# Storing 1100 output columns in the middle of the load queue of a max-pool kernel

## The chip, the cores and the metric

The kernel runs on one core of one Trainium2 chip. The metric is device time in microseconds (us), with a granted clock of 1.0. "Profile" is the page of one profiled execution, "trace" the records behind it, and "packet records" the trace's list of DMA packets with start, duration and size. Times inside an execution are counted from the start of its span, and each run has one profiled execution. The "SP ring" and the "ACT ring" are the queues of the DMAs (transfers) that these two engines issue; the buffer that the kernel calls `ring` is something else. A "row" is one partition's part of a transfer, and is one packet in the records. A "turn" is the place where the stream of loads changes to a store, or back.

## The reference

The reference is an adaptive max pool. With 32 x 256 rows of 4096 floats and 256 outputs per row, each output is the maximum of 16 neighbouring values: 134.22 MB are read, 8.39 MB written.

```python
def reference(x, output_size):
    batch, channels, length = x.shape
    result = np.zeros((batch, channels, output_size), dtype=np.float32)
    for i in range(output_size):
        start = int(i * length / output_size)
        end = int((i + 1) * length / output_size)
        result[:, :, i] = np.max(x[:, :, start:end], axis=-1)
    return result
```

## The kernel before

The outputs form two groups. Each group is spread over 128 partitions and loaded in pieces of up to 1024 windows (16 floats each) into a ring buffer that holds two pieces. VectorE reduces each piece in two parts, 876 (in one piece 872) and 148 columns. The larger is always first: the next load into the same half of the buffer needs its place and not that of the smaller. Results stay on chip in `kept`, and are stored at the end; only the last 836 columns go out on ACT's ring.

```python
    ring = pool.tile([P, 2 * (CHUNK + GAP) * W], fp32, tag="ring", name="ring")
    kept = pool.tile([P, total - last], fp32, tag="kept", name="kept")
    # ... cut ...
    for g, loads in enumerate((group_a, group_b)):
        xg, og = group(sum(loads))
        # ... cut: a first load of 192 windows ...
                low = n_loads % 2 * (CHUNK + GAP)
                moved = n_loads // 2 % 2
                at = low + moved * GAP
                nc.sync.dma_start(out=ring[:, at * W : (at + n) * W], in_=xn)
                # ... cut: pooled(...) of the two parts, or of the last piece ...
                n_loads += 1
            a += n
        full = a - last if g else a
        stores.append((og[:, 0:full], kept[:, base : base + full]))
        base += full

    nc.scalar.dma_start(out=og[:, full : full + last], in_=last_kept)
    tc.no_sync_barrier()
    for dst, src in stores:
        nc.sync.dma_start(out=dst, in_=src)
```

"The eighth load" below is the eighth of the 1024-window loads, the first load of 192 windows not counted.

Of the kernel before, what the change touches and what calls it, by code (L numbers as in the profile page):

```python
# [1 line left out]

# [4 lines left out]


@with_exitstack
def kernel(  # L10
    ctx: ExitStack,
    tc: tile.TileContext,
    x: bass.AP,
    output_size: bass.AP,
    out: bass.AP,
):








    nc = tc.nc
    P = nc.NUM_PARTITIONS
    fp32 = mybir.dt.float32

    B, C, L = x.shape
    O = int(output_size)  # L30
    assert L % O == 0, (L, O)
    W = L // O
    total = B * C * O // P
    assert B * C * O % P == 0

    CHUNK = 1024
    GAP = 148
    FIRST = 192
    LOADS_A, LOADS_B = 9, 6

    LESS = 4
    group_a = [FIRST] + [CHUNK] * (LOADS_A - 1) + [CHUNK - LESS]
    last = total - sum(group_a) - LOADS_B * CHUNK
    group_b = [CHUNK] * LOADS_B + [last]
    assert 0 < last and last * (W + 1) <= CHUNK * W

    pool = ctx.enter_context(tc.tile_pool(name="pool", bufs=1))
    ring = pool.tile([P, 2 * (CHUNK + GAP) * W], fp32, tag="ring", name="ring")
    kept = pool.tile([P, total - last], fp32, tag="kept", name="kept")

    xw = x.flatten_outer_dims().rearrange("r (o w) -> (r o) w", w=W)
    ow = out.flatten_outer_dims().rearrange("r o -> (r o)")

    def pooled(dst, at, n):

        nc.vector.reduce_max(  # L56
            out=dst,
            in_=ring[:, at * W : (at + n) * W].rearrange("p (n w) -> p n w", w=W),
            axis=mybir.AxisListType.X,
        )  # L60

    taken = 0

    def group(n):

        nonlocal taken
        span = slice(taken * P, (taken + n) * P)
        taken += n
        return (
            xw[span].rearrange("(p n) w -> p (n w)", p=P),  # L70
            ow[span].rearrange("(p n) -> p n", p=P),
        )

    stores = []
    n_loads = 0
    base = 0
    for g, loads in enumerate((group_a, group_b)):
        xg, og = group(sum(loads))
        a = 0
        for n in loads:  # L80
            xn = xg[:, a * W : (a + n) * W]
            dst = kept[:, base + a : base + a + n] if n != last else None
            if n == FIRST:

                nc.sync.dma_start(  # L85
                    out=ring[:, CHUNK * W : (CHUNK + n) * W], in_=xn
                )
                pooled(dst, CHUNK, n)
            else:
# [5 lines that stand above are left out]
                if n != last:  # L95
                    cut = CHUNK - GAP if moved else GAP
                    parts = [(0, cut), (cut, n)]
                    for u, v in parts if moved else parts[::-1]:
                        pooled(dst[:, u:v], at + u, v - u)
                else:  # L100
                    end = (at + CHUNK) * W
                    last_kept = ring[:, end - n : end]
                    pooled(last_kept, at, n)
                n_loads += 1
            a += n
        full = a - last if g else a
        stores.append((og[:, 0:full], kept[:, base : base + full]))
        base += full
    assert taken == total

# [6 lines that stand above are left out]
# [1 line left out]
_INS = ['x', 'output_size']  # L118
_OUTS = [((32, 256, 256), 'float32')]

_NUMBERS = {'output_size': 256}


# [26 lines left out]
```

## Time and profile before

| | before |
|---|---|
| time, median | 335.06 us (6 runs, 334.91 to 335.16) |
| DMA share from 20 to 330 us | 1.00, at 432 to 433 GB/s |
| VectorE busy | 276.5 us, 83% |
| first packet of the small store after ACT's issue (packet records) | 1.88 us |
| last packet of all (packet records) | 331.92 us |

The prediction shows most of the lines. The timeline of VectorE: the columns are start, duration, engine, line, operation, output and input with shapes, count, and in brackets the idle time before it and what ended it.

```profile
142.35 17.28 DVE L56 TENSOR_REDUCE kept<-ring 128x876 f32<-128x14016 f32 x2 [2.08 <-DMA ring<-in_x_dram]
161.70 17.28 DVE L56 TENSOR_REDUCE kept<-ring 128x876 f32<-128x14016 f32 x2 [2.07 <-DMA ring<-in_x_dram]
180.97 17.21 DVE L56 TENSOR_REDUCE kept<-ring 128x872 f32<-128x13952 f32 x2 [1.99 <-DMA ring<-in_x_dram]
```

The second line is the eighth load's reduce, the third the ninth's. VectorE waits about 2 us for each load. As the SP ring is never idle, any longer wait here means that the loads themselves came later.

The ninth load in the chain of waits (start, length, what), and what the SP queue waits for at its end (total, times, longest):

```profile
157.13 23.82 DMA ring<-in_x_dram
```

```profile
SPq L145 <- DMA out_dram<-kept: 16.7, 1, 16.7
SPq L145 <- DMA out_dram<-ring: 1.0, 1, 1.0
```

The last two lines say that the large stores land first and the small one 1.0 us after them.

### The profile page before, as it was taken

Reading aid. Unit: us, or ns where it says so; the run is one execution under the profiler, and the core shown is the slowest. Engines: PE = TensorE matmul, PEld = TensorE weight load, DVE = VectorE, ACT = ScalarE, POOL = GpSimd, SP = SyncE. Lnnn points to the kernel's source line nnn. Section 1 sums busy time; section 2 is a strip of 40 time slices with the busy share of each in tenths; the row PEclk is TensorE's granted clock in tenths of the full one; section 3 lists DMA queues with packets and bytes.
Section 4 is the critical chain, followed back from the end, with each engine's and each line's share of the span. In section 5 each row is a group of like instructions: output and inputs, shape, how many; then the busy total and the mean of one; then the engine's idle time right before and its main releaser. Section 6 shows DMA issues by size and latency. Waiting matters only on the chain.

```text
span 333.3 us, 114 instructions
## 1 busy us (share of the span) xinstructions
DVE 276.5 (83%) x32; POOL 0.2 (0%) x4
## 2 busy tenths in 40 slices
DVE  1208979798897979899797979979797997979994
POOL 0000000000000000000000000000000000000000
DMA  8989898998989898999989898999989898989997
GB/s 315 503 378 503 378 496 385 456 425 385 496 378 503 378 503 378 480 401 409 470 376 502 378 503 378 488 393 425 456 378 503 378 503 378 488 353 494 405 401 317
DMA packets 2880, 142.61 MB, mean 428 GB/s; under 512 B 320, under 2 KB 320, under 8 KB 448
## 3 DMA queue, kind: packets, MB, share of 16 engines
q1 hardware_dynamic: 2736, 142.18, 98.8%
q10 hardware_dynamic: 144, 0.43, 0.3%
HBM read 134.22 MB, written 8.39 MB: 428 GB/s over the span
## 4 chain that ended last, share of the span: by engine, by line
DMA 58%; DVE 36%; DVEq 5%; issue 0%; SPq 0%
DMA ring<-in_x_dram 58%; DVE kept L56 36%; DVEq L145 5%; SPq L85 0%
## 5 line engine op out<-in xcount | busy, mean ns | idle before, releaser
L56 DVE TENSOR_REDUCE kept<-ring 128x148 f32<-128x2368 f32 (+3 forms) x31 | 262.5, 8507 | 51.9 <-DMA ring<-in_x_dram 51.9
L56 DVE TENSOR_REDUCE ring<-ring 128x836 f32<-128x13376 f32 x1 | 14.1, 14076 | 0.0
L131 POOL MEMSET const-bfloat16-1.0<- 128x1 bf16 x1 | 0.1, 102 | 0.0
L131 POOL MEMSET const-uint8-127<- 128x1 uint8 x1 | 0.1, 102 | 0.0
L131 POOL MEMSET const-float32-0.0<- 128x1 f32 x1 | 0.1, 99 | 0.2 <-issue 0.2
L131 POOL MEMSET const-float32-1.0<- 128x1 f32 x1 | 0.1, 99 | 0.0
## 6 DMA issues: line engine op xcount, KB each, us to landing
ring<-in_x_dram SPq DMA_DIRECT2D x1, 8160.0 KB, 23.8
ring<-in_x_dram SPq DMA_DIRECT2D x1, 6688.0 KB, 20.4
out_dram<-kept SPq DMA_DIRECT2D x1, 4702.0 KB, 31.2
out_dram<-kept SPq DMA_DIRECT2D x1, 3072.0 KB, 17.0
ring<-in_x_dram SPq DMA_DIRECT2D x1, 1536.0 KB, 6.2
out_dram<-ring ACTq DMA_DIRECT2D x1, 418.0 KB, 4.1
ring<-in_x_dram SPq DMA_DIRECT2D x14, 23.9
```

What stands on the lines that cost most here:

```text
L56: nc.vector.reduce_max(out=dst, in_=ring[:, at * W : (at + n) * W].rearrange("p (n w) -> p n w", w=W), axis=mybir.AxisListType.X,)
L131: nc = _bacc.Bacc("TRN2", target_bir_lowering=False, num_devices=1)
L145: with _tile.TileContext(nc) as tc:
```

## The change

Its intent is evidently to shorten the stores of the tail, by writing 1100 columns (563 KB) while the loads still run.

```diff
+    EARLY, EARLY_AT = 1100, 8
     for g, loads in enumerate((group_a, group_b)):
 ... cut ...
                 n_loads += 1
+                if n_loads == EARLY_AT:
+                    nc.sync.dma_start(out=og[:, 0:EARLY], in_=kept[:, 0:EARLY])
             a += n
         full = a - last if g else a
-        stores.append((og[:, 0:full], kept[:, base : base + full]))
+        done = EARLY if g == 0 else 0
+        stores.append((og[:, done:full], kept[:, base + done : base + full]))
         base += full
```

## The prediction

> **What bounds the kernel now.** I read the page's busy shares first, then the busy time of engines and DMA in three stretches, then the chain of work that ended last, the timeline of the tail, the groups by shape, and last the packet records of the trace.
>
> ```profile
> DVE 276.5 (83%) x32; POOL 0.2 (0%) x4
> ...
> q1 hardware_dynamic: 2736, 142.18, 98.8%
> q10 hardware_dynamic: 144, 0.43, 0.3%
> HBM read 134.22 MB, written 8.39 MB: 428 GB/s over the span
> ```
>
> One compute engine works, VectorE (DVE), at 83% of the span. The load ring q1 carries nearly all bytes, at 98.8% of sixteen DMA engines over the whole span. The next view tells whether the missing 1.2% lies inside the stream or at its ends. Columns: stretch in us, its length, DVE busy, POOL busy, clock, DMA share, GB/s.
>
> ```profile
> 20.00:312.00 292.00, 256.76 (x30) 0.00 (x0) 1.00 1.00 433
> 312.00:330.00 18.00, 16.35 (x2) 0.00 (x0) 1.00 1.00 432
> 328.00:334.00 6.00, 0.35 (x1) 0.00 (x0) 1.00 0.51 211
> ```
>
> From 20 us to 330 us the DMA share is 1.00 at 432 to 433 GB/s, in the loads as in the stores of the tail. What is missing is at the start and after 330 us. The forty-slice row with its 7s, 8s and 9s is misleading here: short slices count a packet as a lump, and longer stretches even this out.
>
> ```profile
> 258.37 14.76 DVE kept L56
> 273.13 0.02 issue
> 273.15 23.91 DMA ring<-in_x_dram
> 297.06 0.02 issue
> 297.08 15.83 DVE kept L56 x2
> 312.91 0.09 issue
> 313.00 15.35 DVEq L145
> ```
>
> This is the end of the chain of waits: reduce, issue of the load that takes the freed half of the buffer, 23.9 us to its landing, reduce. It looks like a latency loop of 14.76 + 23.91 us for two loads, but it is not one. A load of 1024 windows is 8192 KB, 8.39 MB, and lands every 19.34 us, which is 434 GB/s: the DMA rate itself. Each load is issued while its predecessor still has about 4.6 us to go (the load issued at 41.02 us meets one that releases VectorE at 45.60). So there is always work in the ring, and VectorE waits some 2.08 us per load:
>
> ```profile
> 277.73 17.28 DVE L56 TENSOR_REDUCE kept<-ring 128x876 f32<-128x14016 f32 x2 [2.08 <-DMA ring<-in_x_dram]
> 292.89 21.84 SPq L114 DMA_DIRECT2D out_dram<-kept  x2
> 297.08 17.28 DVE L56 TENSOR_REDUCE kept<-ring 128x876 f32<-128x14016 f32 x2 [2.07 <-DMA ring<-in_x_dram]
> 314.28 14.08 DVE L56 TENSOR_REDUCE ring<-ring 128x836 f32<-128x13376 f32 x1
> 328.38 0.37 ACTq L111 DMA_DIRECT2D out_dram<-ring  x1
> ```
>
> The tail has two strands. VectorE reduces the last two loads without a gap (297.08 to 328.36 us), then ACT issues the last small store. Meanwhile the DMA engines write the two large stores. The landing times complete it:
>
> ```profile
> out_dram<-kept SPq DMA_DIRECT2D x1, 4702.0 KB, 31.2
> out_dram<-kept SPq DMA_DIRECT2D x1, 3072.0 KB, 17.0
> ...
> out_dram<-ring ACTq DMA_DIRECT2D x1, 418.0 KB, 4.1
> ```
>
> The 3072 KB store is issued just after 314.4 us and lands near 331.5; the 418 KB store is issued at 328.38 and lands near 332.5. The waits of the SP queue agree: 16.7 us for the large stores, then only 1.0 us more for the small one. **Both strands end within about 1 us of each other**: the kernel has been tuned so that DMA work and the chain through the last reduce run out together.
>
> The packet records sharpen this. Put on the span's clock, the first packet of the small store starts at 330.26 us, the last packet of the 3072 KB store ends at 330.86, the last packet of all at 331.92. All sixteen engines have a packet in flight from about 6 us until after 330. The small store thus arrives while the other ring still has a little queued: no hole, but a slack of only about 0.6 us.
>
> **What the Trainium skill says.** "DMA: Bandwidth & Descriptors", section "Where 436 GB/s comes from", gives a ceiling of 435 GB/s for the SBUF ports and a lower HBM share per core of about 358. The trace, at 433 to 434, agrees with the first; the second does not bind here. The same page, "Queues, rings and completion order", says that each DMA engine consumes a ring's descriptors in ring order, and takes turns between rings packet by packet. In this trace the large stores behind the last load do wait for it (31.2 us to landing for a store that needs some 11). The same page, "Why small descriptors are slow (HBM only)", tells of a fixed cost per packet. The trace has one, though far too small to matter at these row lengths (below).
>
> **The change, part by part.** It adds one store of 1100 columns x 4 B = 4400 B per partition (563 KB over 128 partitions) on the SP queue, right after the eighth 1024-window load. It takes the same 1100 columns out of the 9404-column store of the tail. The instruction order of VectorE is unchanged; SP has one issue more. The early store's data come from the first 192-window load and part of the next, reduced by about 44 us, and it is issued about when its predecessor load is, near 138 us, so it waits for no data. The compiled wait lists show no new wait on a recent event (only semaphores are renumbered; the last load gains a wait on the early store's completion, some 130 us old by then).
>
> *Added in the middle.* Packet records: a row of 65536 B takes 2419 ns, one of 3344 B 135 ns (medians). That is 0.0367 ns per byte and 12 ns fixed. A row of 4400 B then takes 174 ns; 128 rows over 16 engines are 8 each, 1.39 us, with the completion record 1.40 us. The engines have no hole there, and the store stands in the same ring ahead of the ninth load. So **the ninth and every later load land 1.4 us later**. VectorE's 2.07 us wait for that load becomes about 3.5 us, once. It cannot be caught up, since the stream runs at the DMA rate with no idle time.
>
> *Removed at the end.* 4400 B from each of 128 rows of the 9404-column store: 8 x 4400 x 0.0367 = 1.29 us. The work of the DMA engines as a whole grows by only 0.11 us. The large stores then end at nearly the same time as before, slightly earlier because the small store no longer interrupts them.
>
> *The end.* The last load lands 1.4 us later and so does the one before it; the last reduce ends at 329.76 instead of 328.36. ACT's store is issued 1.4 us later, and its first packet starts at 331.66 instead of 330.26. By then the large stores are through: before, the engines finish at about 331.6 us on average, of which the small store is 8 x 135 ns = 1.1 us, so alone the large stores would end near 330.6 after the change. A hole of about 1 us opens. The small store then runs alone, 1.1 us plus some 0.2 us of stagger between engines, instead of 1.66 us from its first packet to its last beside the other ring: 0.3 to 0.4 us gained. Sum: 1.4 - 0.35 = **+1.05 us**. The span becomes about 334.35, the time 335.13 + 1.05 = **336.2 us**, 0.3% slower.
>
> **The rivals.**
>
> *Gain from a shorter tail.* This is the evident intent: 563 KB less to write at the end, up to 1.3 us saved. For it: the large stores occupy the DMA engines until 330.86. Against it: what ends last is the small store, which follows the last reduce, and that waits for loads which the early store delays. It could only gain if the stream had holes for the early store to fill: time 333.9. The share of 1.00 from 20 to 330 us says there are none.
>
> *Hidden anyway.* A write and a read might overlap in an engine (different directions), so that the early store costs the loads less than 1.4 us. For it: VectorE's own slack of 2.07 us per load, which is of no use as the loads are the pace. Against it: in the tail 4702 KB go out in about 11.2 us (312.9 to 324.1), 430 GB/s, no faster than loads, and the engines' rate is already at the ceiling. Time 335.2 to 335.6.
>
> *A turn-around cost.* A load behind a store in the same ring may start with a bubble, or small rows may do worse beside loads; the trace has the turn from load to store (no bubble: the 37616 B rows all take 1392 to 1425 ns) but never from store to load. At perhaps 0.5 us: time 336.7.
>
> *VectorE becomes the bound.* It would need its 2.07 us wait to vanish; the change lengthens it.
>
> **Range and chances.** Fully serial without relief at the end is +1.4 us (336.5), with a bubble 336.9; hidden in part is 335.5. All lie within 0.6% of the time before, and its runs differ by 0.06 us, though another session may shift by some tenths. Low 335.6, high 336.8. For 2% either way 6.7 us are needed, five times the cost of the whole store: faster 0.01, same 0.98, slower 0.01.
>
> **What would show it.** Right: the ninth load's wait on VectorE grows from 2.07 to near 3.5 us and later ones stay at 2.0 to 2.1; every reduce after it starts 1.4 us later; the last ACT issue is near 329.8; the small store takes under 4.1 us to landing; SP's final wait for it, after the large stores, grows from 1.0 to about 2.3 us. Wrong: if the later reduces have not shifted, the early store found free DMA time; if they shift by 2 us or more, turning costs time; if the small store still takes 4.1 us or more, the relief of 0.35 us fails.

## The result and the profile after

The changed kernel takes **336.00 us** in the median (335.76 to 336.11, 6 runs), the kernel before 335.06. The ratio is 1.0028 (95% interval 1.0015 to 1.0041): 0.94 us slower, within 2%. Ratios here are the mean time of one kernel's fast runs over that of the other's of the same rounds, so not quite the ratio of the medians. The profiled execution of the changed kernel happened to be its fastest run (335.76), so its span shows +0.7 us (334.0 against 333.3).

Timeline of VectorE in the changed kernel, same columns:

```profile
142.23 17.28 DVE L56 TENSOR_REDUCE kept<-ring 128x876 f32<-128x14016 f32 x2 [2.07 <-DMA ring<-in_x_dram]
...
162.17 17.28 DVE L56 TENSOR_REDUCE kept<-ring 128x876 f32<-128x14016 f32 x2 [2.66 <-DMA ring<-in_x_dram]
182.77 17.21 DVE L56 TENSOR_REDUCE kept<-ring 128x872 f32<-128x13952 f32 x2 [3.32 <-DMA ring<-in_x_dram]
202.12 17.28 DVE L56 TENSOR_REDUCE kept<-ring 128x876 f32<-128x14016 f32 x2 [2.13 <-DMA ring<-in_x_dram]
...
316.08 14.07 DVE L56 TENSOR_REDUCE ring<-ring 128x836 f32<-128x13376 f32 x1
330.18 0.37 ACTq L115 DMA_DIRECT2D out_dram<-ring  x1
```

The ninth load's wait grows by 1.33 us and then all is as before, as foreseen. But the *eighth* load, which stands ahead of the store in the ring, comes 0.59 us late as well. Together the brackets read 5.98 us, 1.92 more than before; the loads never catch up, and ACT issues the small store at 330.18 instead of 328.38, +1.80.

The ninth load in the chain of waits, 25.74 us from release to landing against 23.82:

```profile
157.01 25.74 DMA ring<-in_x_dram
```

The end is milder. The landing times and the SP queue's last waits:

```profile
out_dram<-kept SPq DMA_DIRECT2D x1, 3072.0 KB, 15.7
...
out_dram<-ring ACTq DMA_DIRECT2D x1, 418.0 KB, 2.9
```

```profile
SPq L149 <- DMA out_dram<-kept: 15.4, 1, 15.4
SPq L149 <- DMA out_dram<-ring: 1.1, 1, 1.1
```

The small store takes 2.9 us to landing instead of 4.1, and still lands only 1.1 us behind the large ones. So both strands of the tail still end together: the hole of 1 us that the prediction saw between them is not there.

The packet records say where both deviations lie. Ahead of the early store, the last row of 65536 B on each of the sixteen engines takes 3.09 us in the mean, where such rows take 2.42. The store's own rows take 171 ns each, eight per engine, 1.37 us. In the tail, the small store's first packet starts 0.88 us after ACT's issue (331.06) instead of 1.88, and the last packet of all ends at 332.59 instead of 331.92.

### The profile page after: what moved, and what is told of

Its sections match the earlier page's. It is cut to its first block, busy times and chain, and to the rows that moved or that the text cites. A ratio compares the mean times of both kernels' runs of the same rounds, so it can differ in the third digit from the quotient of the medians.

```text
span 334.0 us, 115 instructions
## 1 busy us (share of the span) xinstructions
DVE 276.5 (83%) x32; POOL 0.2 (0%) x4
## 4 chain that ended last, share of the span: by engine, by line
DMA 58%; DVE 36%; DVEq 5%; issue 0%; SPq 0%
DMA ring<-in_x_dram 58%; DVE kept L56 36%; DVEq L149 5%; SPq L86 0%
```

## The experiments

Two questions were open. Why does the store cost the loads 1.92 us where its packets take 1.37? And what sets the end: the chain through the last reduce with its fixed delay, as predicted, or the total work of the DMA engines? "Excess" below is the growth of VectorE's waits around the store over the store's own packets; in the changed kernel it is 1.92 - 1.37 = 0.55 us. Three theories were tried for it: A, a fixed cost of every turn from load to store; B, an excess that grows with the bytes; C, a gap of limited length. Two rivals to all were that any short rows, or the place in the schedule, are to blame.

### Size: 128, 2200 and 5000 columns

```diff
-    EARLY, EARLY_AT = 1100, 8
+    EARLY, EARLY_AT = 128, 8      # e128; 2200 in e2200, 5000 in e5000
```

> The early store has only 128 columns (rows of 512 B) instead of 1100; the rest of it stays in the tail. Measure: start of the last reduce less start of the first 876-column reduce (288.04 us before, 289.97 after: +1.93). Theory A, a fixed cost at the turn from load to store and back, about 0.6 us whatever the size: +0.6 and 8 rows of about 31 ns (0.25), so +0.8, and the rows of 65536 B just ahead of the store are stretched to about 3.1 us as in the changed kernel; time about 335.7. Theory B, the excess grows with the bytes stored: +0.3 to +0.4, no stretched rows beyond 2.5 us, time about 335.2.

> The early store has 2200 columns (rows of 8800 B, 335 ns each by the line through the packet records, 8 per engine: 2.7 us). Theory A, fixed turn cost: loads after it shift by 2.7 + 0.6 = 3.3 us; Theory B, excess with bytes: 3.8. For the end: if all that counts is the DMA engines' total work (they are never idle until the last packet), the time stays where the changed kernel is, about 336.0; if the chain through the last reduce counts, its small store now finds the engines idle and starts about 0.9 us after its issue, and the time is that of before + 3.3 - 1.2 = 337.1, with a hole ahead of the small store in the packet records.

> The early store with 5000 columns (rows of 20000 B, 746 ns each, 8 per engine: 6.0 us). So far the excess of the shift over the store's own packets is about 0.05 us or less for 128 columns, 0.6 for 1100, 1.05 for 2200. Theory B (excess with the bytes, about 0.4 of the store's own time): shift 8.3 us. Theory C (a gap of limited length, once the store is long enough to drain what the engines hold ahead): excess about 1.1, shift 7.1 us. Time: the small store runs alone behind the last reduce, so before + shift - 1.3: 342.1 (B) or 340.9 (C).

VectorE's waits for the eighth and ninth load, with 128, 2200 and 5000 columns:

```profile
161.78 17.28 DVE L56 TENSOR_REDUCE kept<-ring 128x876 f32<-128x14016 f32 x2 [2.18 <-DMA ring<-in_x_dram]
181.26 17.21 DVE L56 TENSOR_REDUCE kept<-ring 128x872 f32<-128x13952 f32 x2 [2.20 <-DMA ring<-in_x_dram]
```

```profile
162.60 17.28 DVE L56 TENSOR_REDUCE kept<-ring 128x876 f32<-128x14016 f32 x2 [3.20 <-DMA ring<-in_x_dram]
184.47 17.21 DVE L56 TENSOR_REDUCE kept<-ring 128x872 f32<-128x13952 f32 x2 [4.59 <-DMA ring<-in_x_dram]
```

```profile
162.46 17.28 DVE L56 TENSOR_REDUCE kept<-ring 128x876 f32<-128x14016 f32 x2 [3.05 <-DMA ring<-in_x_dram]
187.77 17.21 DVE L56 TENSOR_REDUCE kept<-ring 128x872 f32<-128x13952 f32 x2 [8.04 <-DMA ring<-in_x_dram]
```

| store | growth of the two waits | own packets | excess | mean of the rows ahead | time (before, same rounds) |
|---|---|---|---|---|---|
| 128 columns | 0.32 us | 0.22 | 0.10 | 2.43 us | 335.12 (335.08) |
| 1100, the change | 1.92 | 1.37 | 0.55 | 3.09 | 336.00 (335.06) |
| 2200 | 3.73 | 2.66 | 1.07 | 3.33 | 336.85 (335.08) |
| 5000 | 7.03 | 5.95 | 1.08 | 3.20 | 340.04 (335.08) |

Theory A fell with 128 columns: no stretched rows, and an excess of 0.10 us, which is no more than the scatter of the other waits in that execution (2.04 to 2.22). The measure for it, from the first large reduce to the last, reads +0.62 (288.66 against 288.04), between the two forecasts. Of it 0.32 stand at the store and the rest at other loads (waits of 2.13, 2.21 and 2.22), where nothing was changed; the table therefore counts the two waits alone. That execution was the slowest of its four (335.44). Theory B, with its slope taken from the first three sizes, fell with 5000 columns: growth 7.03, not 8.3. What the sizes support is C: a gap that is absent for a small store and does not exceed some 1.1 us for a large one, in one execution each. The time with 5000 columns, 340.04, is below both forecasts (342.1 and 340.9): the end was again reckoned too late.

The larger stores also show what the prediction took to be the end of the changed kernel. With 2200 columns the packet records have a real hole: the large stores' last packet ends at 331.80, the small store's first starts at 332.76, 0.87 us after ACT's issue. Here the chain through the last reduce does set the end, and further delay is paid nearly in full: from 2200 to 5000 columns the waits grow by 3.30 us and the time by 3.19. With 1100 columns the point where this begins has not been reached.

### Direction: a load, and a copy on the chip, of the same rows

```diff
-                    nc.sync.dma_start(out=og[:, 0:EARLY], in_=kept[:, 0:EARLY])
+                    nc.sync.dma_start(
+                        out=kept[:, 14000 : 14000 + EARLY], in_=xg[:, 0:EARLY]
+                    )                     # ldmid; in_=kept[:, 0:EARLY] in sb2sb
 ... cut ...
-        done = EARLY if g == 0 else 0
+        done = 0
```

> In place of the early store, a needless load of the same 1100 columns' worth of bytes per partition (rows of 4400 B) into columns that are overwritten later; the tail keeps its full store. Result stays right. Theory A (turn between reading and writing costs 0.6): no turn here, loads shift by 1.4 us, no stretched rows. Rival (any DMA of short rows put between two loads costs the extra 0.6): shift 1.9 and stretched rows. The end: nothing is taken from the tail, so DMA work grows by 1.4 us as a whole and the time is 336.4 to 336.5 without turn cost, about 337.0 with it.

> In place of the early store, a needless copy of the same 4400 B rows from one place of on-chip memory to another (columns overwritten later); tail full. If reading on-chip memory between two loads is what costs the 0.6: shift 1.9 to 2.0 and stretched rows ahead. If it is the writing to HBM: shift 1.35 to 1.4 as for the needless load, no stretched rows. Time 336.4 without, 337.0 with the excess.

The needless load, then the needless copy on the chip:

```profile
161.52 17.28 DVE L56 TENSOR_REDUCE kept<-ring 128x876 f32<-128x14016 f32 x2 [2.07 <-DMA ring<-in_x_dram]
182.15 17.21 DVE L56 TENSOR_REDUCE kept<-ring 128x872 f32<-128x13952 f32 x2 [3.35 <-DMA ring<-in_x_dram]
```

```profile
162.22 17.28 DVE L56 TENSOR_REDUCE kept<-ring 128x876 f32<-128x14016 f32 x2 [2.72 <-DMA ring<-in_x_dram]
182.82 17.21 DVE L56 TENSOR_REDUCE kept<-ring 128x872 f32<-128x13952 f32 x2 [3.33 <-DMA ring<-in_x_dram]
```

The needless load behaves exactly as the prediction had the store: the wait for the load ahead is untouched (2.07), the one behind grows by 1.36, own packets 1.37, excess zero, time 336.36 against 335.08. The copy on the chip behaves as the store does: +1.99 in all, excess 0.62, rows ahead 3.23 us, time 337.07. So neither short rows nor writing to HBM are needed for the excess; a block of reads from on-chip memory between two loads is enough (or of transfers that do not read HBM, which is the same set here). The times of all runs say it too: the copy costs 0.71 us more than the load (337.07 against 336.36).

### No load behind: the same store in the tail

```diff
-    for dst, src in stores:
-        nc.sync.dma_start(out=dst, in_=src)
+    for g, (dst, src) in enumerate(stores):
+        cut = 1100 if g == 0 else 0
+        if cut:
+            nc.sync.dma_start(out=dst[:, 0:cut], in_=src[:, 0:cut])
+        nc.sync.dma_start(out=dst[:, cut:], in_=src[:, cut:])
```

> The kernel before with its 9404-column store of the tail cut into 1100 and 8304 columns, both issued in the tail one behind the other. Only the turn from load to a store of 4400 B rows is as in the changed kernel; no load follows. If short rows right after a load are what stretches the load's last rows: those of 53504 B take about 2.6 us instead of at most 1.985, and the time is about 335.7. If the turn costs only where another load stands behind the store: rows as before and time 335.1 to 335.2.

335.21 us against 335.08. Some of the last load's rows were longer (at most 2.40 us against 1.99), but summed over rows this is 0.11 us per engine. So without a load behind it the store has little excess. But a load behind is not strictly needed for longer rows: in the profiled execution of actring, below, the last rows of the last load were longer by 0.47 us per engine, although its tail is that of the changed kernel, which had none of it. This part varies between executions.

### The end alone: the change without the turn

```diff
 (the needless load of ldmid, and)
-        done = 0
+        done = EARLY if g == 0 else 0
```

> The needless load of 4400 B rows in the middle AND the tail without its first 1100 columns (never stored: the result is incomplete on purpose). This is the changed kernel without the turn: loads 1.35 us later, tail 1.29 us shorter. The prediction's reckoning of the end (small store's first packet 1.9 us after its issue, a hole of 1 us): time of before + 1.05 = 336.1. The rival (first packet 0.9 us after issue once the other ring is nearly done, so no hole, and the end set by the DMA engines' total work): + 0.1 to + 0.3, 335.2 to 335.4.

335.23 us against 335.08, +0.15; the 1100 columns are never stored, so the result is incomplete. The loads are late by 1.37 us, and the end hardly moves. In its packet records the small store starts 0.88 us after ACT's issue (330.53) while the large stores end at 330.85: no hole. **The rival in the expectation was right and the prediction's reckoning of the end was wrong**: up to this size the end follows the total work of the DMA engines, not the chain through the last reduce. Most of the time that the changed kernel loses is then due to the turn: 0.94 - 0.15 = 0.79 us by the medians, where its profiled execution, the fastest, shows 0.55 us in the waits and 0.67 in the rows.

### Two stores of half the size

```diff
-    EARLY, EARLY_AT = 1100, 8
+    EARLY, EARLY_AT = 1100, {7: 0, 9: 550}      # apart: 550 columns each
```

In the run called pairback, both halves stand one behind the other after the eighth load instead.

> The 1100 columns in two early stores of 550 columns, one behind the seventh load and one behind the ninth. Own packets 8 rows of 93 ns twice, 1.5 us. Theory B (excess with bytes): the two together shift the loads by 1.5 + 0.5 = 2.0. If a store of few bytes hides its excess (128 columns showed none), less: 1.5 to 1.7, and then the time falls to 335.5 or so, below the 336.0 of the changed kernel.

> The 1100 columns behind the eighth load in two stores of 550 columns, one right behind the other. Measure: VectorE's waits for the eighth and ninth load, together 4.06 us before, 5.98 in the changed kernel. Stores of 550 columns a load apart had no excess over their own packets. If what counts is the bytes that stand between two loads (35 KB per engine here, as in the changed kernel): own packets 1.43 + 0.55 = 2.0 us more, waits 6.0, rows ahead stretched, time about 336.0. If what counts is the single store or its row length: 1.43 more, waits 5.5, time about 335.4.

The waits for the eighth, ninth and tenth load with the halves a load apart, then for the eighth and ninth with the halves back to back:

```profile
162.37 17.28 DVE L56 TENSOR_REDUCE kept<-ring 128x876 f32<-128x14016 f32 x2 [2.71 <-DMA ring<-in_x_dram]
181.65 17.21 DVE L56 TENSOR_REDUCE kept<-ring 128x872 f32<-128x13952 f32 x2 [2.00 <-DMA ring<-in_x_dram]
201.73 17.28 DVE L56 TENSOR_REDUCE kept<-ring 128x876 f32<-128x14016 f32 x2 [2.87 <-DMA ring<-in_x_dram]
```

```profile
162.19 17.28 DVE L56 TENSOR_REDUCE kept<-ring 128x876 f32<-128x14016 f32 x2 [2.74 <-DMA ring<-in_x_dram]
183.41 17.21 DVE L56 TENSOR_REDUCE kept<-ring 128x872 f32<-128x13952 f32 x2 [3.94 <-DMA ring<-in_x_dram]
```

A load apart, the waits for the eighth, ninth and tenth load were 2.71, 2.00 and 2.87, 1.39 more than before, for 1.43 us of own packets: no excess. The time was 335.49 (335.08 before), half of the loss regained. Back to back they cost more than one store of 1100: waits 2.74 and 3.94, +2.62 for 1.42 us of packets, an excess of 1.20, and 336.41 us (334.98 before). Neither expectation had that. Part of it stands behind the store: the first rows of the ninth load take 2.65 us in the mean, against 2.41. What stands between two loads as one block counts, but its bytes alone do not give the size; the second DMA, or the doubled number of rows, adds to it. Which, was not tested.

### The other ring, and the place in the schedule

```diff
-                    nc.sync.dma_start(out=og[:, 0:EARLY], in_=kept[:, 0:EARLY])
+                    nc.scalar.dma_start(out=og[:, 0:EARLY], in_=kept[:, 0:EARLY])   # actring
```

ACT issues as soon as the data are ready, near 44 us, between other loads than SP did. Therefore sp3 has the store on the SP ring at that same time (`EARLY_AT = 3`).

> The early store of 1100 columns goes out on the ACT ring, as soon as its data are ready (about 44 us), row by row in turns with the loads of the SP ring. If the excess comes with every turn between a read of HBM and a read of on-chip memory: 8 turns per engine, up to 8 x 0.55 us more. If it comes only where the store drains what the engine has read ahead: single rows of 4400 B among rows of 65536 B do not, the loads shift by 1.4 us in all and the time is that of the run without a turn, about 335.2 to 335.3: the better way to store early.

> The changed kernel with its early store behind the third load instead of the eighth, still on the SP ring: issued about 44 us, as the store on the ACT ring was. If it is the ring (the whole store standing in one block between two loads) that costs the excess, it is there as before: VectorE's waits for the third and fourth load together grow from 4.14 us by about 1.9, rows of 65536 B stretched to about 3.1 us, time about 336.0. If it was the place in the schedule that spared the ACT ring's store, the waits grow by 1.4 only and the time is 335.2 to 335.3.

The third and fourth load's reduces, ACT ring first, SP ring second:

```profile
66.07 17.28 DVE L56 TENSOR_REDUCE kept<-ring 128x876 f32<-128x14016 f32 x2 [3.41 <-DMA ring<-in_x_dram]
85.37 17.28 DVE L56 TENSOR_REDUCE kept<-ring 128x876 f32<-128x14016 f32 x2 [2.03 <-DMA ring<-in_x_dram]
```

```profile
65.84 17.28 DVE L56 TENSOR_REDUCE kept<-ring 128x876 f32<-128x14016 f32 x2 [2.99 <-DMA ring<-in_x_dram]
86.50 17.28 DVE L56 TENSOR_REDUCE kept<-ring 128x876 f32<-128x14016 f32 x2 [3.38 <-DMA ring<-in_x_dram]
```

On the ACT ring the two waits grow by 3.41 + 2.03 - 4.14 = 1.30 us, no more than the store's packets. In the packet records its rows are spread from 46.96 to 65.65 us, between the rows of the loads, and none of those rows is stretched. On the SP ring they grow by 2.23, an excess of 0.86, with rows ahead of 3.2 to 3.5 us. Times: 335.24 (334.98 before) and 335.91 (335.06 before). So the early place in the schedule did not spare the ACT store: the SP store at the same time has the excess, and its loss (0.85 us) is about that of the changed kernel (0.94). What spared it is the other ring, or that its rows stood singly there and not in one block; the two were not tried apart. The ACT version is the best way found to store these 1100 columns early, and it only comes close to the kernel before: no run beat that, and since its sixteen engines are busy until the end, an early store has nothing to win here.

## Why the prediction was right or wrong

- **The bound, and that nothing hides the store**: right. The later reduces shifted and never caught up; the gain from a shorter tail and the hidden store did not happen.
- **The total, +1.05 us (336.2)**: right in size (+0.94, 336.00), but by luck: it is the difference of two terms that were both too small, 1.4 for the delay (1.80 at ACT's issue) and 0.35 for the relief (1.12), so that the errors cancelled in part.
- **"the ninth and every later load land 1.4 us later"**: the term for the store's own packets was right (171 ns a row against 174 estimated). It left out the excess of 0.55 us, which arrives with the eighth load, ahead of the store: +1.92 us of waits in place of 1.4. The prediction had it as a rival, "a turn-around cost" of perhaps 0.5 us, but looked for it behind the store and took no part of it into the sum. Its sign for it, reduces shifted by 2 us or more, stood just above the 1.80 that came.
- **"A hole of about 1 us opens"**: this step failed. It carried the 1.88 us from ACT's issue to the first packet over from the kernel before, as if it were fixed. It is 0.88 once the other ring has little left, and 0.87 in e2200, where the other ring is empty. The relief at the end was 1.80 - 0.68 = 1.12 us (shift of ACT's issue less shift of the last packet), not 0.35. The forecast that SP's last wait would grow to 2.3 us was the test of it, and it stayed at 1.1.
- **The reading that replaces it**: the DMA engines' total work sets the end. It grew by the row overhead (0.1 us) and the stretched rows (3.09 - 2.42 = 0.67 us), 0.77 in all, against +0.68 at the last packet, in an execution whose first large reduce happened to start 0.13 us earlier (26.11 against 26.24). Without the turn, ldswap shows +0.15. Had the prediction sized the end rightly and left the turn out, it would have said 335.2 and been further off.
- **A small misreading**: the 2.07 us that the prediction gives as the ninth load's wait is the eighth's; the ninth's is 1.99, and it grew to 3.32, not 3.5.
- **Left open**: why a block of on-chip reads slows the last rows of the load ahead. The runs show when (a block of 1100 columns or more, or two of 550 together, on the ring of the loads) and how much (0.55 to 1.2 us), not the mechanism; that engines read ahead and run dry, as two expectations suppose, no run shows. Where in the ring the time is really lost is open too, since the packet records may book it on the row ahead.

## What to carry to other kernels

When the DMA engines are busy from end to end, moving a store earlier moves no work away; ask instead what the move adds. A block of stores between loads on one ring added 0.55 to 1.2 us of its own; here short blocks, or single rows on the other ring, avoided it. And an issue-to-first-packet delay read beside other traffic is partly a wait for that traffic: do not carry it over to a state where the traffic is gone.

## What the Trainium skill lacked or had wrong

- "DMA: Bandwidth & Descriptors" has nothing on a store or an on-chip copy standing between loads on one ring. Measured: no excess for 550 columns (2200 B rows) that stand alone, 0.55 us for 1100, 1.07 for 2200, 1.08 for 5000, 1.20 for two stores of 550 together, 0.62 for an on-chip copy of 1100, and none for a load of the same rows.
- The same page, "Issuing engines are not separate DMA queues", says that initiating on several engines "will only save the time on the sequencer it takes to initiate the DMA". Here the same store at the same time cost +0.26 us on the ACT ring and +0.85 on the SP ring; the issue itself took 0.35 us on SP (43.52 us) and held up no load, as the next was not issued before 60.35.
- The same page, "Where 436 GB/s comes from", has the HBM side (about 358 GB/s per core) bind transfers between HBM and on-chip memory. This core moved 433 GB/s for 292 us, near the 435 of the ports. The same passage calls its own measured 425 near the rate of the fabric, so what does not hold here is only the flat sentence that the HBM side binds.
